# Output products in written order, transposes a token tile later, and a residual added by VectorE

## The chip, the cores and the metric

The kernel runs on one core of a Trainium2 chip. The core has five engines that run their own instruction streams: TensorE (PE in the profile, with PEld for its weight loads), VectorE (DVE), ScalarE (ACT), GpSimd (POOL) and SyncE (SP, which issues most DMAs). They wait for each other by semaphores. The metric is the time of one execution on the device in microseconds (us), a median over several runs. All work is for one sequence of 512 tokens.

## The reference, cut to what matters

An encoder trunk of four layers: gated DeltaNet (GDN), an MLP, gated linear attention (GLA) and a second MLP. After each of them stands a residual sum and a layer normalisation over the 1024 channels.

```python
for i in range(DEPTH):                        # DEPTH = 2
    j = i // N_MIXERS
    if i % N_MIXERS == 0:
        m = _mixer_gdn(x, a_w_in[j], a_conv[j], a_alog[j], a_dt_bias[j], a_norm_g[j], a_w_out[j])
    else:
        m = _mixer_gla(x, b_w_in[j], b_gate_w2[j], b_gate_b[j], b_norm_g[j], b_w_out[j])
    x = _layernorm(DEEPNORM_ALPHA * x + m, ln1_g[i], ln1_b[i])
    x = _layernorm(DEEPNORM_ALPHA * x + _sq_relu_mlp(x, mlp_w1[i], mlp_w2[i]), ln2_g[i], ln2_b[i])
```

Both mixers begin with a product of x with `w_in` (projections), run a recurrence per head in both directions, normalise the head's output, gate it, and end with a product with `w_out` (the output product). The MLP is `relu(x @ w1)**2 @ w2` with 4096 features.

## The kernel before, in words

**Tiles.** The 512 tokens are four token tiles (`NT` = 4) of 128 rows, `xt0` to `xt3`, each 128 x 1024 in fp32. A half tile is 512 of the 1024 columns. Projections want x with channels on the partitions; so each finished token tile is transposed on TensorE: `xpose` (L146) makes two groups (`q` = 0, 1) of four 128x128 transposes, each into one PSUM bank named `tp`; ScalarE copies the bank to `xth` (L149) and VectorE subtracts that copy from the bank into `xtl` (L150). The pair is a high and a low part: an fp32 product is made as three matmuls by `mm3` (L109 high by high, L110 and L111 the cross terms).

**Stages.** In the trace GDN runs from 0 to about 437 us, the first MLP (MLP0) to about 788, GLA to about 1056 and the second MLP (MLP1) to 1401. The transposes at the end of a stage and the first projections of the next are called a seam here. The projections that begin a stage (`proj_halves`) are made in two halves of 256 tokens: all of them for token tiles 0 and 1 first, then for tiles 2 and 3.

**Output product of a mixer.** Most heads' part of the output product is made early and summed with alpha times x into `z` (`out_part`, `out_pieces`; in GLA z lies in the `xt` tiles themselves). The last heads' part is `out_last`: for each token tile and half it opens a bank `ob`, puts z into it with a matmul by the identity (L241, the residual matmul), and adds the products with `w_out`. In GDN these are two heads, 6 and 7, each one `mm3` of 512 columns; in GLA they are two heads of two blocks each, four `mm3`. Head 7 is the last to be ready in GDN: `fo` (L1364, VectorE) is transposed into `otp` (L1368), gated into `p` (L1370), and split in `oh` (L1371, ScalarE) and `ol` (L1372, VectorE). In GLA the last head goes from `o` (L791) by `otp` (L795) to `oth` (L798) and `otl` (L799).

**Layer normalisation.** `layernorm` takes the two half tiles: statistics (L184, L185), the inverse root (L159 to L165, two steps of it on ScalarE), a subtract and multiply for each half (L188), and a multiply and add: on VectorE for the first half (L191), on ScalarE and GpSimd for the second (L193, L194). With `last=True` the second half too is finished on VectorE.

**MLP.** It begins with four features' projections (`specs`, by `proj_halves`), then single ones (`feature`), and has its hidden features in four groups. The last group's product with `w2` is `last`: banks `pl`, eight `mm3` for each half tile, the first four with the high and low parts of one hidden half and the other four with those of the other (`ah`, `al`, made on ScalarE and VectorE at L90 and L91), then the sum into x (L320, VectorE), layernorm, and the transposes for the next stage, into the banks `pj`.

**What sets the order.** A scheduler orders the instructions of each engine by their dependencies and its own estimates, unless a stretch of the program stands under `in_order(engine)`, which chains all instructions of that engine in the order in which they are written. PSUM is divided anew in each stage: GDN has 1 bank `tp`, 2 `ac` and 3 `pj`, GLA 2 `tp`, 2 `ac` and 4 `pj`, the MLPs 2 each of `pj`, `X`, `Y` and `Z`.

Of the kernel before, what the change touches and what calls it, by code (L numbers as in the profile page):

```python
# [8 lines left out]
F32 = mybir.dt.float32  # L9
# [8 lines left out]
P = 128  # L18
# [10 lines left out]
class Ctx:  # L29
# [109 lines left out]
    def xpose(self, t, src, tags=("tp",)):  # L139

        nc = self.nc
        for q in range(2):
            ps = self.bank([P, 4, P], F32, name="tp", tag=tags[(2 * t + q) % len(tags)])
            for i in range(4):
                k = 4 * q + i
                nc.tensor.transpose(ps[:, i, :], src[:, k * P:(k + 1) * P], self.ident)  # L146
            hi = self.xth[:, 4 * q:4 * q + 4, t * P:(t + 1) * P]
            lo = self.xtl[:, 4 * q:4 * q + 4, t * P:(t + 1) * P]
            last = nc.scalar.copy(hi, ps)  # L149
            nc.vector.tensor_tensor(lo, ps, hi.bitcast(F32), ALU.subtract)  # L150
        return last

# [78 lines left out]
    def out_last(self, w, ks, lhs, z, tags, par, homes=None, xtags=("tp",)):  # L231

        nc = self.nc
        homes = iter(homes or [None] * len(ks))
        ws = [[self.wrows(w, k * P, hf * 512, next(homes)) for k in ks[::2]] for hf in range(2)]
        for t in range(NT):
            sl = slice(t * P, (t + 1) * P)
            pss = []
            for hf in range(2):
                ps = self.bank([P, 512], F32, name="ob", tag=tags[(2 * t + hf) % len(tags)])  # L240
                nc.tensor.matmul(ps, self.ident, z[t][hf], start=True, stop=False)  # L241
                for i, k in enumerate(ks):
                    ah, al = lhs(k, sl)
                    wh, wl = ws[hf][i // 2]
                    self.mm3(ps, ah, al, wh[:, i % 2, :], wl[:, i % 2, :], False, i == len(ks) - 1)
                pss.append(ps)
            self.layernorm(pss, self.xh(t), par)
            self.xpose(t, self.xt[t], xtags)


def mlp(c, w1, w2, g, b, out=None, extra=None):
# [13 lines left out]
    with c.banks(pj=2, X=2, Y=2, Z=2), tc.tile_pool(name="mlp", bufs=2) as pool:  # L265
# [133 lines left out]
        def last(gi, h):  # L399

            a = {}
            for i in range(2):
                for j in range(2):
                    a[i, j] = pair(h[j][:, :, HT * i:HT * i + HT], "raw" if i else "ah")
            ws = [c.wrows(w2, (gi * GF + 2 * (i % 4)) * P, i // 4 * 512, pool=ring("w2") if i < 3 else None if i < 6 else ring("raw"))
                  for i in range(8)]
            if out is None:
                c.new_x()
            for t in range(NT):
                sl = slice(t % 2 * P, t % 2 * P + P)  # L410
                for hf in range(2):
                    ps = c.bank([P, 512], F32, name="pl", tag="XYZ"[(2 * t + hf) % 3])
                    for k in range(GF):
                        wh, wl = ws[4 * hf + k // 2]
                        ah, al = a[t // 2, k // HF]
                        c.mm3(ps, ah[:, k % HF, sl], al[:, k % HF, sl], wh[:, k % 2, :], wl[:, k % 2, :], k == 0, k == GF - 1)
                    add(t, hf, ps)
                c.layernorm(c.xh(t), c.xh(t), par, last=out is not None)
                if out is None:
                    c.xpose(t, c.xt[t], ("pj",))  # L420
                else:
                    nc.sync.dma_start(out[t * P:(t + 1) * P, :], c.xt[t])
# [3 lines left out]
        for f, ps in enumerate(c.proj_halves(specs)):  # L426
            act(ps, h[0][:, f, :])
# [80 lines left out]
def gla(c, gc, w_in, gate_w2, w_out, ln_g, ln_b):  # L508
# [5 lines left out]
    with c.banks(ac=2, tp=2, pj=4), tc.tile_pool(name="gla", bufs=2) as pool:  # L514
# [11 lines left out]
        gps, *qk0 = c.proj_halves(specs)  # L526
# [19 lines left out]
        with c.in_order(mybir.EngineType.PE):  # L546
# [18 lines left out]
            for h in range(H):  # L565
                for s in level:
# [12 lines left out]
        c.out_last(w_out, list(range(KT // 2, KT)), lhs, z, ("pj",), par,  # L579
                   [None, (pool, "v", "sr", 2), (pool, "F", "F", 2), (pool, "v", "sr", 2)])  # L580
# [384 lines left out]
def gdn(c, w_in, conv_w, a_log, dt_bias, norm_g, w_out, ln_g, ln_b, x):  # L965
    tc, nc = c.tc, c.nc
    with c.banks(ch=2, pj=3, tp=1, ac=2), tc.tile_pool(name="gdn", bufs=1) as pool:
# [37 lines left out]
        c.out_last(w_out, [6, 7], lhs, z, ("ac", "pj"), par)  # L1005
# [375 lines left out]
def body(tc, nc, a, out):  # L1381
    with contextlib.ExitStack() as es:
# [5 lines left out]
        gdn(c, a["a_w_in"][0], a["a_conv"][0], a["a_alog"][0], a["a_dt_bias"][0], a["a_norm_g"][0],  # L1388
            a["a_w_out"][0], a["ln1_g"][0], a["ln1_b"][0], x)
        with tc.tile_pool(name="gcst", bufs=1) as gp:  # L1390
            gc = []
            mlp(c, a["mlp_w1"][0], a["mlp_w2"][0], a["ln2_g"][0], a["ln2_b"][0],
                extra=lambda tmp: gc.append(GlaConst(c, gp, a["b_gate_b"][0], a["b_norm_g"][0], tmp)))
            gla(c, gc[0], a["b_w_in"][0], a["b_gate_w2"][0], a["b_w_out"][0], a["ln1_g"][1], a["ln1_b"][1])
        mlp(c, a["mlp_w1"][1], a["mlp_w2"][1], a["ln2_g"][1], a["ln2_b"][1], out=out[0])
# [18 lines left out]
```

## Time and profile before

| | |
|---|---|
| median of three runs | 1403.77 us (1403.65 to 1403.82) |
| span of the profiled execution, first to last instruction | 1401.7 us |
| busy TensorE / VectorE / ScalarE / GpSimd in it | 1366.0 / 929.5 / 689.5 / 121.3 us |
| mean granted TensorE clock | 0.998 |
| residual matmuls (L241) | 16 in GDN and 16 in GLA as the trace counts them, two to a half tile |
| transposes of x (L146) | 128 matmuls, 21.0 us shown |

The profiled execution's own time isn't given apart from its span; the median lies 2.1 us over the span, time before the first and behind the last instruction.

How to read the rows. A row of the timeline has the start in us from the span's start, the duration in us, engine, line, operation, output<-inputs, partitions x elements and a count; in brackets stands how long the engine was idle before and what released it. Matmuls are pipelined: each is shown from its start to its modelled end, so successive ones overlap and their distance from start to start is what they cost. A row of the waits has the waiting engine, output and line, what it waited for, us in all, times, and the longest. A row of the windows has the stretch and its length, then the busy time of PE, PEld, DVE, ACT and POOL, each with its count, the granted clock (1.00 is full), the DMA share and GB/s.

### The profile page before, as it was taken

The numbers are of one execution on the slowest core, as the hardware profiler recorded it, in microseconds if no ns is written. First come the engines' busy times: TensorE is split into PE (matmuls) and PEld (weight loads), VectorE is DVE, ScalarE is ACT, GpSimd is POOL, SyncE is SP. The second block draws the span as 40 slices with busy tenths as digits, with TensorE's granted clock in tenths as the row PEclk, the third lists the DMA queues.
The fourth block names the chain that finished last, engine by engine and source line by source line (L and its number), as shares of the span: only waits on it lengthen the run. The fifth ranks groups of instructions, "written<-read, shape, count | busy, mean of one in ns | idle before, by whom it ended". The sixth has DMA issues, their size and how long they took to land.

```text
span 1401.7 us, 20232 instructions
## 1 busy us (share of the span) xinstructions
PE 1366.0 (97%) x7933; PEld 1116.8 (80%) x7933; DVE 929.5 (66%) x1541; ACT 689.5 (49%) x1320; POOL 121.3 (9%) x168
## 2 busy tenths in 40 slices
PE   7999999999999999999999999999999999999997
PEld 6777777777777888888887888888878888888886
DVE  5787787778667365655556577877764655656655
ACT  3776657666633454444543354554433644445430
POOL 5000000000003300100000100000002000001000
PEclk9999999999999999999999999999999999999999
DMA  6212111211133964655431222222217666656121
GB/s 171 76 48 59 46 46 46 61 46 46 47 111 96 291 154 148 144 155 120 105 96 44 85 86 73 61 61 61 89 47 225 178 183 150 165 120 134 48 83 52
DMA packets 153030, 142.23 MB, mean 101 GB/s; under 512 B 8399, under 2 KB 123207, under 8 KB 152935
## 3 DMA queue, kind: packets, MB, share of 16 engines
q1 hardware_dynamic: 144112, 111.49, 26.5%
q0 software_dynamic: 8256, 29.37, 10.8%
q8 instruction: 62, 1.02, 0.3%
q14 instruction: 33, 0.27, 0.1%
q10 hardware_dynamic: 567, 0.08, 0.0%
HBM read 113.66 MB, written 2.10 MB: 83 GB/s over the span
## 4 chain that ended last, share of the span: by engine, by line
PE 59%; issue 23%; DMA 6%; ACT 6%; POOL 3%; DVE 2%; SPq 1%; DVEq 0%; POOLq 0%; ACTq 0%
DMA w2r<-w2r 4%; PE pj L109 3%; PE pj L111 3%; PE pj L110 3%; PE pjv L109 3%; PE pjv L111 3%; PE pjv L110 3%; PE scp L688 2%; DMA w2r<-in_mlp_w 2%; PE op L1345 2%; PE pjq L110 1%; PE pjq L111 1%; PE pjq L109 1%; PE op L776 1%; PE lv L1220 1%
## 5 line engine op out<-in xcount | busy, mean ns | idle before, releaser
L91 DVE TENSOR_TENSOR wl<-wst,wh 128x1024 fp32r<-128x1024 f32 x137 | 168.5, 1230 | 194.0 <-ACT wh L90 193.3
L90 ACT CAST wh<-wst 128x1024 fp32r<-128x1024 f32 x137 | 144.0, 1051 | 282.7 <-PE pj L110 170.2
L109 PE MATMUL pj<-xth,wh 128*128 128x512 f32 (+1 forms) x544 | 202.0, 372 | 1.7 <-ACT h L276 0.9
L111 PE MATMUL pj<-xth,wl 128*128 128x512 f32 (+1 forms) x544 | 201.7, 371 | 0.4 <-DVE wl L91 0.4
L110 PE MATMUL pj<-xtl,wh 128*128 128x512 f32 (+1 forms) x544 | 201.6, 371 | 0.4 <-DVE xtl L150 0.3
L91 DVE TENSOR_TENSOR w2l<-w2r,w2h 128x1024 fp32r<-128x1024 f32 x84 | 102.6, 1221 | 68.3 <-ACT w2h L90 68.3
L109 PEld LDWEIGHTS pj<-xth,wh 128*128 128x128 f32 x544 | 102.2, 188 | 20.4 <-ACT h L276 2.3
L110 PEld LDWEIGHTS pj<-xtl,wh 128*128 128x128 f32 x544 | 102.5, 188 | 18.6 <-DVE xtl L150 0.8
L111 PEld LDWEIGHTS pj<-xth,wl 128*128 128x128 f32 x544 | 102.4, 188 | 18.6 <-DVE wl L91 0.8
L90 ACT CAST w2h<-w2r 128x1024 fp32r<-128x1024 f32 x84 | 88.2, 1050 | 57.2 <-DMA w2r<-in_mlp_w 25.5
L303 POOL DMA_DIRECT2D w2r<-w2r x48 | 41.5, 902 | 398.2 <-DVE w2l L91 230.1
L90 ACT CAST ah<-h 128x1024 fp32r<-128x1024 f32 x40 | 42.1, 1054 | 42.1 <-PE pX L110 16.8
L110 PE MATMUL pX<-w2l,ah 128*128 128x512 f32 x144 | 56.1, 390 | 0.0
L109 PE MATMUL pX<-w2h,ah 128*128 128x512 f32 x144 | 56.1, 390 | 0.0
L111 PE MATMUL pX<-w2h,al 128*128 128x512 f32 x144 | 56.1, 390 | 0.0
L109 PE MATMUL pjv<-wh,xth 128*128 128x512 f32 x128 | 54.9, 429 | 0.0
L91 DVE TENSOR_TENSOR al<-h,ah 128x1024 fp32r<-128x1024 f32 x40 | 48.9, 1222 | 5.3 <-ACT ah L90 3.7
L160 ACT ACTIVATE rsy<-rsv 128x1 f32<-128x1 f32 (+1 forms) x28 | 5.6, 201 | 90.9 <-DVE rsv L159 90.9
L111 PE MATMUL pjv<-wh,xtl 128*128 128x512 f32 x128 | 50.2, 392 | 0.0
L110 PE MATMUL pjv<-wl,xth 128*128 128x512 f32 x128 | 49.9, 390 | 0.0
L1168 POOL TENSOR_TENSOR atl<-on,ath 128x512 f16<-128x512 f32 x16 | 20.9, 1306 | 323.4 <-ACT ath L1167 171.5
L109 PE MATMUL pjk<-xth,wh 128*128 128x512 f32 (+1 forms) x112 | 42.1, 376 | 0.5 <-ACT wh L90 0.5
(439 smaller groups left out, 3443.3 us busy)
## 6 DMA issues: line engine op xcount, KB each, us to landing
wst<-in_mlp_w SPq DMA_DIRECT2D x80, 512.0 KB, 4.0
w2r<-in_mlp_w SPq DMA_DIRECT2D x48, 512.0 KB, 4.3
w2r<-w2r POOLq DMA_DIRECT2D x48, 512.0 KB, 5.6
wst<-in_a_w_in SPq DMA_DIRECT2D x32, 512.0 KB, 4.0
wst<-in_b_w_in SPq DMA_DIRECT2D x32, 256.0 KB, 3.0
wst<-in_a_w_out SPq DMA_DIRECT2D x8, 512.0 KB, 3.8
wst<-in_b_w_in SPq DMA_DIRECT2D x8, 512.0 KB, 3.7
wst<-in_b_w_out SPq DMA_DIRECT2D x8, 512.0 KB, 3.6
```

Source lines behind the costliest of these rows:

```text
L90: nc.scalar.copy(hi, src)
L91: nc.vector.tensor_tensor(lo, src, hi.bitcast(F32), ALU.subtract)
L109: mm(ps, ah, bh, start=start, stop=False, **kw)
L110: mm(ps, ah, bl, start=False, stop=False, **kw)
L111: mm(ps, al, bh, start=False, stop=stop, **kw)
L160: nc.scalar.activation(y, v, AF.Ln)
L303: nc.gpsimd.dma_start(blocks[a + (q,)], blocks[b + (q,)], accum_op=ALU.add)
L688: T.matmul(ps[:, n, :], kh[:, sl], qh[:, sl], start=True, stop=True)
L776: T.matmul(ops, l, r, start=i == 0, stop=i == len(mm) - 1)
L1168: G.tensor_tensor(atl[:, us, :], at, ath[:, us, :], ALU.subtract)
L1220: T.matmul(ps[:, u, :, :], lhs[:, u, :], cols(rhs, u, s, i), start=True, stop=True)
L1345: T.matmul(op[:, n, :], l, r, start=i == 0, stop=i == len(mm) - 1)
```

## The change

1. `out_last` runs under `in_order` for TensorE, in both mixers. A tile's transposes are written `late` tiles later: one tile in GLA, two in GDN. It returns the tiles whose transposes are left (GDN: 2 and 3; GLA: 3). The last tile's layernorm is finished on VectorE.
2. The MLP makes the transposes that are left (`left`) between the projections of its first features, by `between` in `proj_halves`, into the banks `Y` and `Z`: the last tile's before `k` = 0 and 4 of the third feature, an earlier one's before `k` = 4 and 7 of the first, all in the pass over tiles 0 and 1.
3. The MLP's `last` runs under `in_order` for TensorE. In MLP0 the transposes of tile t-1 stand in the middle of tile t's second half; tile 3's stand between the projections of GLA, before `k` = 0 and 4 of `pjk`, and its layernorm is finished on VectorE. MLP1 keeps its stores and has no transposes.
4. In GLA `out_last` is called with `add=True`: no residual matmul, the first product opens the bank, and VectorE adds the bank to z.

The diff, without the signatures that only pass these on:

```diff
-    def proj_halves(self, specs):
+    def proj_halves(self, specs, between=None):
...
+        between = between or {}
...
-            for ps, ((wh, wl), _, _) in zip(out, specs):
+            for i, (ps, ((wh, wl), _, _)) in enumerate(zip(out, specs)):
                 n = wh.shape[-1]
                 for k in range(KT):
+                    if hf == 0 and (i, k) in between:
+                        between[i, k]()
...
+    def xposes(self, t, *tags):
+
+        src = self.xt[t]
+        return [lambda q=q, tag=tag: self.xpose(t, src, (tag,), (q,)) for q, tag in enumerate(tags)]
...
-    def out_last(self, w, ks, lhs, z, tags, par, homes=None, xtags=("tp",)):
+    def out_last(self, w, ks, lhs, z, tags, par, homes=None, xtags=("tp",), add=False, late=1):
...
+        with self.in_order(mybir.EngineType.PE):
+            for t in range(NT):
+                sl = slice(t * P, (t + 1) * P)
+                pss = []
+                for hf in range(2):
+                    ps = self.bank([P, 512], F32, name="ob", tag=tags[(2 * t + hf) % len(tags)])
+                    if not add:
+                        nc.tensor.matmul(ps, self.ident, z[t][hf], start=True, stop=False)
+                    for i, k in enumerate(ks):
+                        ah, al = lhs(k, sl)
+                        wh, wl = ws[hf][i // 2]
+                        self.mm3(ps, ah, al, wh[:, i % 2, :], wl[:, i % 2, :], add and i == 0, i == len(ks) - 1)
+                    if add:
+                        nc.vector.tensor_tensor(z[t][hf], z[t][hf], ps, ALU.add)
+                    pss.append(z[t][hf] if add else ps)
+                self.layernorm(pss, self.xh(t), par, last=t == NT - 1)
+                if t >= late:
+                    self.xpose(t - late, self.xt[t - late], xtags)
+        return [t for t in range(NT - late, NT)]
...
+            with c.in_order(mybir.EngineType.PE):
+                for t in range(NT):
+                    sl = slice(t % 2 * P, t % 2 * P + P)
+                    for hf in range(2):
+                        ps = c.bank([P, 512], F32, name="pl", tag="XYZ"[(2 * t + hf) % 3])
+                        for k in range(GF):
+                            if out is None and t and hf and k == HF:
+                                c.xpose(t - 1, c.xt[t - 1], ("pj",))
...
+                    c.layernorm(c.xh(t), c.xh(t), par, last=out is not None or t == NT - 1)
...
+        between = {}
+        for j, t in enumerate(left):
+            for q, run in enumerate(c.xposes(t, "Y", "Z")):
+                between[(2, 4 * q) if j == len(left) - 1 else (0, 4 + 3 * q)] = run
+        with c.in_order(mybir.EngineType.PE):
+            halves = c.proj_halves(specs, between)
...
-        gps, *qk0 = c.proj_halves(specs)
+        with c.in_order(mybir.EngineType.PE):
+            gps, *qk0 = c.proj_halves(specs, dict(zip(((2, 0), (2, 4)), c.xposes(NT - 1, "tp", "tp"))))
...
+        return c.out_last(w_out, list(range(KT // 2, KT)), lhs, z, ("pj",), par,
+                          [None, (pool, "v", "sr", 2), (pool, "F", "F", 2), (pool, "v", "sr", 2)], add=True)
...
+        return c.out_last(w_out, [6, 7], lhs, z, ("ac", "pj"), par, late=2)
```

In the changed kernel the lines move: L146, L149, L150 become L149, L152, L153; L184 and L188 become L192 and L196; L241 becomes L251; L1364 and L1368 become L1386 and L1390; L791 and L795 become L813 and L817. VectorE's new add is L257.

Where GDN's output product begins, TensorE's instructions stand as follows before (`ob` is a half tile's bank, `z` the residual, `oh3` and `ol_421` head 6, `oh3` with `ol_422` head 7, `otp` the transposes of head 7):

```order
L241 MATMUL ob_5666<-z_5265,ident_70 128x512
...
L111 MATMUL ob_5666<-wh_5656,ol_421 128x512
L241 MATMUL ob_5674<-z_5506,ident_70 128x512
...
L111 MATMUL ob_5674<-wh_5662,ol_421 128x512
L241 MATMUL ob_5717<-z_5265,ident_70 128x512
...
L110 MATMUL ob_5717<-wl_5657,oh3_414 128x512
L1368 MATMUL otp_5631<-ident_70,fo_5629 128x128 x4
L111 MATMUL ob_5717<-wh_5656,ol_421 128x512
L241 MATMUL ob_5725<-z_5506,ident_70 128x512
...
L109 MATMUL ob_5666<-wh_5656,oh3_414 128x512
```

In the changed kernel the same stretch begins so:

```order
L251 MATMUL ob_5666<-z_5265,ident_70 128x512
L109 MATMUL ob_5666<-wh_5656,oh3_414 128x512
L110 MATMUL ob_5666<-wl_5657,oh3_414 128x512
L111 MATMUL ob_5666<-wh_5656,ol_421 128x512
L1390 MATMUL otp_5631<-ident_70,fo_5629 128x128 x4
L109 MATMUL ob_5666<-wh_5656,oh3_414 128x512
L110 MATMUL ob_5666<-wl_5657,oh3_414 128x512
L111 MATMUL ob_5666<-wh_5656,ol_422 128x512
L251 MATMUL ob_5674<-z_5506,ident_70 128x512
```

Four half tiles' residual and head 6 products stood ahead of the first product of head 7; now one half tile's do, and the transposes into `otp` come right behind it.

The transposes of GDN's first token tile (`xt0`, two groups of four) stand like this on TensorE before, inside the products of a later half tile:

```order
L111 MATMUL ob_5776<-wh_5662,ol_422 128x512
L241 MATMUL ob_5819<-z_5265,ident_70 128x512
L146 MATMUL tp_5703<-ident_70,xt0_5650 128x128 x4
L109 MATMUL ob_5819<-wh_5656,oh3_414 128x512
L110 MATMUL ob_5819<-wl_5657,oh3_414 128x512
L111 MATMUL ob_5819<-wh_5656,ol_421 128x512
L109 MATMUL ob_5819<-wh_5656,oh3_414 128x512
L110 MATMUL ob_5819<-wl_5657,oh3_414 128x512
L111 MATMUL ob_5819<-wh_5656,ol_422 128x512
L241 MATMUL ob_5827<-z_5506,ident_70 128x512
L146 MATMUL tp_5710<-ident_70,xt0_5650 128x128 x4
L109 MATMUL ob_5827<-wh_5662,oh3_414 128x512
```

And in the changed kernel, behind tile 2's last product (`ob_5748`):

```order
L111 MATMUL ob_5748<-wh_5662,ol_422 128x512
L149 MATMUL tp_5777<-ident_70,xt0_5650 128x128 x4
L149 MATMUL tp_5784<-ident_70,xt0_5650 128x128 x4
L251 MATMUL ob_5791<-z_5265,ident_70 128x512
L109 MATMUL ob_5791<-wh_5656,oh3_414 128x512
L110 MATMUL ob_5791<-wl_5657,oh3_414 128x512
```

The two groups stood eight instructions apart and now follow each other.

Where GLA's output product begins, TensorE's instructions before (`F` and `v` are the places of other weight halves, `o` the last head's output):

```order
L241 MATMUL ob_10490<-xt0_5650,ident_70 128x512
...
L111 MATMUL ob_10490<-wh_10468,otl_8458 128x512
L241 MATMUL ob_10504<-xt0_5650,ident_70 128x512
...
L111 MATMUL ob_10504<-F_10480,otl_8458 128x512
L795 MATMUL otp_10450<-ident_70,o_10417 128x128
...
L795 MATMUL otp_10457<-ident_70,o_10431 128x128
L241 MATMUL ob_10553<-xt1_5651,ident_70 128x512
L109 MATMUL ob_10490<-v_10474,oth_8457 128x512
```

In the changed kernel:

```order
L109 MATMUL ob_10488<-wh_10466,oth_8441 128x512
...
L111 MATMUL ob_10488<-wh_10466,otl_8442 128x512
L817 MATMUL otp_10448<-ident_70,o_10415 128x128
...
L817 MATMUL otp_10455<-ident_70,o_10429 128x128
L109 MATMUL ob_10488<-v_10472,oth_8441 128x512
```

The residual matmuls are gone, and the second half tile's first six products now stand behind the transposes of `o`.

More of the change, by code (lines that the diff above doesn't have):

```diff
@@ L137, in new_x, with xpose @@
         self.xtl = self.big.tile([P, KT, S], F32R, name="xtl", tag="xtl")
-    def xpose(self, t, src, tags=("tp",)):
+    def xpose(self, t, src, tags=("tp",), qs=(0, 1)):
         nc = self.nc
-        for q in range(2):
+        for q in qs:
             ps = self.bank([P, 4, P], F32, name="tp", tag=tags[(2 * t + q) % len(tags)])
@@ L235, in out_last, with mlp @@
         ws = [[self.wrows(w, k * P, hf * 512, next(homes)) for k in ks[::2]] for hf in range(2)]
[L236 to L251, printed above, removed]
+        with self.in_order(mybir.EngineType.PE):
[17 more added lines that the diff above has]
+        return [t for t in range(NT - late, NT)]
+def mlp(c, w1, w2, g, b, left, out=None, extra=None):
     tc, nc = c.tc, c.nc
@@ L1391, in body @@
             gc = []
[L1392 removed]
+            mlp(c, a["mlp_w1"][0], a["mlp_w2"][0], a["ln2_g"][0], a["ln2_b"][0], left,
                 extra=lambda tmp: gc.append(GlaConst(c, gp, a["b_gate_b"][0], a["b_norm_g"][0], tmp)))
[L1394 to L1395 removed]
+            left = gla(c, gc[0], a["b_w_in"][0], a["b_gate_w2"][0], a["b_w_out"][0], a["ln1_g"][1], a["ln1_b"][1])
+        mlp(c, a["mlp_w1"][1], a["mlp_w2"][1], a["ln2_g"][1], a["ln2_b"][1], left, out=out[0])
 def kernel(**inputs):
```

27 lines of the change are left out of this document (8 added, 19 removed).

## The prediction

> **What bounds the kernel now.** I read the page first (busy shares, the row of the granted clock), then the list of waits on TensorE alone in the three stretches in which a stage ends (417 to 456.6, 737 to 797 and 1020 to 1065 us), then the timeline there.
>
> ```profile
> PE 1366.0 (97%) x7933; PEld 1116.8 (80%) x7933; DVE 929.5 (66%) x1541; ACT 689.5 (49%) x1320; POOL 121.3 (9%) x168
> ...
> PEclk9999999999999999999999999999999999999999
> ```
>
> TensorE is busy 97% of the span at the full clock, so time is won or lost only where it waits, or does work that another engine could do. The waits in the three stretches (us in all, times, longest):
>
> ```profile
> PE tp L146 <- DVE xtl L150: 1.3, 2, 0.7
> PE tp L146 <- DVE rst L164: 1.2, 2, 0.8
> PE pj L109 <- ACT xth L149: 0.7, 1, 0.7
> ...
> PE tp L146 <- POOL xt L194: 2.5, 4, 0.7
> PE pjq L109 <- DVE xt L320: 0.9, 1, 0.9
> ...
> PE tp L146 <- POOL xt L194: 1.8, 4, 0.6
> ...
> PE pj L110 <- DVE xtl L150: 0.3, 1, 0.3
> ```
>
> Such a listed wait is not the whole loss, as the start of the output product of the first MLP shows:
>
> ```profile
> 737.01 0.39 PE L109 MATMUL pl<-w2h,ah 128*128 128x512 f32 x1
> 737.24 0.40 PE L110 MATMUL pl<-w2l,ah 128*128 128x512 f32 x1
> ```
>
> A matmul of 512 columns starts 0.23 us after the one before and is shown 0.39 long, so each listed wait costs 0.16 more. The seams then cost 3.2+5x0.16=4.0 us (GDN to MLP0), 3.4+5x0.16=4.2 (MLP0 to GLA) and 2.1+5x0.16=2.9 (GLA to MLP1). These 11.1 us are all that moving transposes can win.
>
> **The change part by part.** *GDN's output product, now in written order.*
>
> ```profile
> 417.01 1.02 PE L241 MATMUL ob<-z,ident 128*128 128x512 f32 x2
> 418.56 1.02 PE L241 MATMUL ob<-z,ident 128*128 128x512 f32 x2
> ...
> 420.69 0.69 DVE L1364 TENSOR_TENSOR fo<-op,ors 128x512 f32<-128x512 f32 x1
> 421.45 0.64 PE L1368 MATMUL otp<-ident,fo 128*128 128x128 f32 x4
> 422.98 0.62 ACT L1371 CAST oh<-p 128x512 fp32r<-128x512 f32 x1 [4.73 <-DVE p L1370]
> 423.63 0.69 DVE L1372 TENSOR_TENSOR ol<-p,oh 128x512 fp32r<-128x512 f32 x1 [0.69 <-ACT oh L1371]
> 423.66 0.50 PE L109 MATMUL ob<-wh,oh 128*128 128x512 f32 x1
> ```
>
> Until head 7 is ready at 423.66, TensorE now does the residual and head-6 part of four half tiles from 417.01 on, 1.55 us each (417.01 to 418.56). In the new order head 7's transposes stand behind one half tile, and everything behind them waits for them. VectorE's order up to `ol` is unchanged, so `otp` still starts at 421.45 and head 7's product at 423.66. TensorE idles from 418.56 and again behind `otp`, and three half tiles, 3x1.55=4.65 us of work, are left over. The third matmul then also waits for `ol` (to 424.32, against a turn 0.46 behind 423.66). That makes +4.8, with little doubt in it (4.6 to 5.2).
>
> *GDN's transposes.* Removed: the 4.0. Added:
>
> ```profile
> 433.37 0.68 DVE L184 BATCH_NORM_STATS2 bst<-ob 128x6 f32<-128x512 f32 x1
> ...
> 434.82 0.60 PE L146 MATMUL tp<-ident,xt 128*128 128x128 f32 x4
> ...
> 436.03 0.73 DVE L188 SCALAR_TENSOR_TENSOR xt<-ob,bmv,lnp 128x512 f32<-128x512 f32 x1
> 436.69 0.67 DVE L150 TENSOR_TENSOR xtl<-tp,xth 128x512 fp32r<-128x512 f32 x1
> ...
> 437.42 0.66 PE L146 MATMUL tp<-ident,xt 128*128 128x128 f32 x4 [0.61 <-DVE xtl L150]
> ```
>
> This stage has one `tp` bank, so a tile's second four transposes wait until the first four are copied and subtracted. Before, matmuls stood between the two (434.82 to 437.42) and the wait left was 0.7 at most; now, for tile 0, nothing stands there. VectorE decides how long it is: tile 2's statistics and both its L196 stand ahead of that subtraction, 0.68+2x0.73+0.67=2.8 and small steps after tile 2's last matmul, a wait of about 3.1. Tile 1's pair, with one `pj` matmul between and two weight splits in VectorE's way, I put at 2.8. Each can be from 0.7 (as now) to 3.1: 1.4 to 6.2 for both. I take 5.9, near the upper end, because the order sets it and not a chance of timing: net +1.9 (-2.6 to +2.2). Tiles 2 and 3 go between projections that need only tiles 0 and 1: nothing.
>
> *MLP0's first features.* Waits at 457 to 490 us:
>
> ```profile
> PE pj L109 <- ACT h L276: 0.9, 2, 0.6
> PE pj L111 <- DVE wl L91: 0.4, 1, 0.4
> ...
> 483.63 1.05 ACT L90 CAST wh<-wst 128x1024 fp32r<-128x1024 f32 x1 [4.81 <-DMA wst<-in_mlp_w]
> ```
>
> They come from weights that arrive late: 1.3+3x0.16=1.8. TensorE gets there 4.8+1.9=6.7 us later. The loads that crowd these weights start with the last layernorm, which comes later by 4.8+3.1, less two thirds of the removed waits (2.7) and the transposes of two tiles (4x0.44): about 3.4. So the weights gain some 3.3 us on TensorE and most of the wait goes: -1.5 (-1.8 to 0). On SP two more `w2r` loads stand ahead of feature 7's weights; these have the same 3.3 us. In MLP1 the reverse holds, since TensorE comes earlier and the last layernorm does not: +0.5 (0 to 1.8, the same wait).
>
> *MLP0's last product.* Removed: the 4.2, as the transposes now come half a product later; the next stage starts with `gps`, which I leave 0.3 for its first wait. Added: the order no longer hops over late operands.
>
> ```profile
> 740.30 1.22 DVE L91 TENSOR_TENSOR al<-h,ah 128x1024 fp32r<-128x1024 f32 x1 [0.50 <-ACT ah L90]
> ```
>
> The second half's `ah` is there when that row starts, at 740.3, and `al` when it ends, at 741.5. TensorE would want `ah` 12 matmuls behind 737.01, at 739.77, and `al` two or three matmuls behind that: waits of 0.5 and 0.7. Before, other matmuls filled this. Net -4.2+0.3+1.2=-2.7 (-3.6 to -2.5). MLP1 has the same edit without transposes: +1.2 (1.0 to 1.4).
>
> *GLA's output product: the residual on VectorE, and written order.*
>
> ```profile
> 1020.94 1.02 PE L241 MATMUL ob<-xt,ident 128*128 128x512 f32 x2
> ...
> 1024.46 1.67 DVE L791 SCALAR_TENSOR_TENSOR o<-o,rs,sr 128x256 f32<-128x256 f32 x4
> 1025.88 1.07 PE L795 MATMUL otp<-ident,o 128*128 128x128 f32 x8 [0.30 <-DVE o L791]
> 1026.56 1.27 ACT L798 ACTIVATE oth<-otp,gcol 128x512 fp32r<-128x512 f32 x2 [2.93 <-PE otp L795]
> 1027.31 1.40 DVE L799 SCALAR_TENSOR_TENSOR otl<-otp,gcol,oth 128x512 fp32r<-128x512 f32 x2
> ...
> 1038.78 1.02 PE L241 MATMUL ob<-xt,ident 128*128 128x512 f32 x2
> ...
> 1042.42 1.02 PE L241 MATMUL ob<-xt,ident 128*128 128x512 f32 x2
> ...
> 1044.10 0.65 PE L146 MATMUL tp<-ident,xt 128*128 128x128 f32 x4 [0.23 <-POOL xt L194]
> ...
> L320 DVE TENSOR_TENSOR xt<-xt,pl 128x512 f32<-128x512 f32 x16 | 10.9, 684 | 25.5 <-PE pl L111 25.5
> ```
>
> A half tile takes 3.64 us (1038.78 to 1042.42), 12x0.23 of it products: a residual costs 0.86. Two of the eight lie ahead of `otp`, which waits for `o` either way; the other six save 6x0.86=5.2. The second half tile's six early matmuls move behind `otp`: +1.4, with TensorE idle from 1020.94+1.4=1022.3 to 1025.9. Then `oth` (0.6 a half, from 1026.56) and `otl` (to 1028.0) are waited for with nothing beside them: +0.9. The eight adds, 0.68 each, are 5.5 us on VectorE. The transposes' 2.9 goes, but a tile now lasts 24x0.23=5.6, while layernorm takes 5.3 from the tile's last product to the second half's transposes (1038.78 to 1044.10) and has one add, 0.68, more ahead of it: 0.4 short at each of three tiles, and up to 1.2 where VectorE is taken. I take 0.8, in the middle, since VectorE is busy 25 of 35 us there (below): +2.4. Net -5.2+1.4+0.9-2.9+2.4=-3.4 (-5.5 to -1).
>
> *The granted clock.* Stretches of busy time (TensorE first, clock and DMA share last but one):
>
> ```profile
> 436.00:439.41 3.41, 1.96 (x10) 1.04 (x8) 3.41 (x11) 2.24 (x5) 1.19 (x1) 1.00 0.00 0
> 1391.73:1395.14 3.41, 0.81 (x4) 0.35 (x2) 2.45 (x7) 0.41 (x2) 0.00 (x0) 1.00 0.00 0
> 1395.15:1398.56 3.41, 0.00 (x0) 0.00 (x0) 2.47 (x7) 0.00 (x0) 0.00 (x0) 0.50 0.00 0
> 1021.00:1056.00 35.00, 33.46 (x145) 23.89 (x144) 25.47 (x54) 11.49 (x25) 3.79 (x3) 1.00 0.18 48
> ```
>
> After a stretch of 3.41 us with 0.81 us of TensorE work the clock was halved; one with 1.96 kept it. The new idle stretches hold less than 1.96: 418.6 to 423.7 has one `otp` (0.6 of 5.1), 1022.3 to 1025.9 nothing. If the clock is decided by fixed stretches of that length, each idle stretch fills one far enough for a drop in about half of all positions. A drop costs half of the next 3.4 us of work, 1.7; the waits in GDN's transposes may cause more of them (0 to +7 in all). I take one drop of the two, +1.7.
>
> [...]
>
> Sum: 4.8+1.9-1.5+0.5-2.7+1.2-3.4+1.7=+2.5 on a span of 1401.7. The median of the runs is 1403.8, so 2.1 us lie around the span, which stay. Forecast: 1403.8+2.5=1406.3.
>
> **Rivals.** *A, the clock holds.* The idle stretches don't lower the grant: 1406.3-1.7=1404.6. [...] Against it: the end of this trace. *B, faster: head 7's chain sets no wait.* Place: between `op` and `oh` in GDN. If `oh` came by 418.6, where the first half tile's early part ends, instead of 423.6, written order would cost nothing there and the clock would hold: 1406.3-4.8-1.7=1399.8. It decides from about 420.5 on. For it: the chain is 3 us of work spread over 420.3 to 423.6, and an order on TensorE alone can change when VectorE gets its operands. Against it: the rows of this chain all stand ahead of the first changed row on VectorE. *C, VectorE bounds GLA's output.* It is busy 25.5 of 35 us there; with 5.5 more in some 31 us it is full. Then that part wins nothing, and its waits bring one more drop: 1406.3+3.4+1.7=1411.4. For it: the arithmetic. Against it: the adds are spread over four tiles.
>
> **Numbers.** Forecast 0.50 (its own range 1404.6 to 1409.7, none to three drops), A 0.20, B 0.18, C 0.12. About 0.2%, 2.8 us, is what a measurement tells from no change here: slower means above 1406.6, faster below 1401.0. More than half of the forecast's range and all of C lie above: 0.28+0.12=0.40. The rest of the forecast and A are the same: 0.22+0.20=0.42. B is faster: 0.18. The range takes in B's point and leaves out C and what lies beyond B: 1399.5 to 1410.5.
>
> **What would show it.** Right: no residual matmul in GLA; TensorE waiting 2 to 4 us for `fo` and again for `o`; the subtraction ending a wait of 2 to 3 us between GDN's halves; a granted clock under 1.00 behind 421 or behind 1025 us. Wrong: those waits under 1 us, waits of over 1 us at each tile of the MLPs' output products, or a clock of 1.00 all through with the time above 1408.

## The result, and the profile after

The changed kernel takes 1412.2 us (median of 4 runs, 1411.4 to 1412.8) against 1403.7 before: a ratio of 1.0056, 95% interval 1.0044 to 1.0068. It is 8.5 us slower; the forecast was 2.5 slower, and the time lies outside the stated range. The profiled execution has a span of 1410.3 us at a mean clock of 0.992 (before 1401.7 at 0.998).

The page of the changed kernel, busy shares and the row of the clock:

```profile
PE 1364.3 (97%) x7917; PEld 1119.7 (79%) x7917; DVE 934.5 (66%) x1552; ACT 687.4 (49%) x1317; POOL 116.5 (8%) x165
...
PEclk9999999999998999999999999999999999999999
```

TensorE has 16 matmul records less (the residuals of GLA), and the row of the clock has a slice under 9. Its waits at the end of GDN, at MLP0's first features, at the end of MLP0, at GLA's output and at MLP1's first features (the end of MLP1 lists the same two rows as the end of MLP0):

```profile
PE tp L149 <- DVE rst L172: 2.9, 1, 2.9
PE otp L1390 <- DVE fo L1386: 2.7, 1, 2.7
PE ob L109 <- ACT oh L1393: 1.6, 1, 1.6
PE tp L149 <- DVE rst L171: 1.3, 1, 1.3
PE pj L109 <- ACT xth L152: 1.2, 1, 1.2
...
PE pj L111 <- DVE wl L91: 2.1, 1, 2.1
PE pj L110 <- DVE xtl L153: 0.6, 1, 0.6
...
PE pl L111 <- DVE al L91: 0.5, 1, 0.5
PE pl L109 <- ACT ah L90: 0.4, 1, 0.4
...
PE otp L817 <- DVE o L813: 3.4, 1, 3.4
PE tp L149 <- POOL xt L202: 1.5, 3, 0.6
PE ob L109 <- ACT oth L820: 0.3, 1, 0.3
PE tp L149 <- DVE xt L199: 0.2, 1, 0.2
...
PE pj L109 <- ACT h L290: 1.8, 1, 1.8
```

Before, no wait here was over 0.9 us. Now four are over 2: for head 7's `fo`, for the subtraction between the two groups of tile 0's transposes (the list names the small step right behind it, `rst`), for the low part `wl` of weights in MLP0, and for GLA's `o`. The timeline shows the first two of them, and that VectorE's chain to `fo` kept its place (`fo` at 420.69 before):

```profile
418.24 0.40 PE L111 MATMUL ob<-wh,ol 128*128 128x512 f32 x1
421.34 0.66 PE L1390 MATMUL otp<-ident,fo 128*128 128x128 f32 x4 [2.71 <-DVE fo L1386]
423.56 0.79 PE L109 MATMUL ob<-wh,oh 128*128 128x512 f32 x1 [1.56 <-ACT oh L1393]
424.15 0.63 PE L110 MATMUL ob<-wl,oh 128*128 128x512 f32 x1
424.57 0.63 PE L111 MATMUL ob<-wh,ol 128*128 128x512 f32 x1
...
440.54 1.09 PE L149 MATMUL tp<-ident,xt 128*128 128x128 f32 x4 [2.93 <-DVE rst L172]
...
420.59 0.69 DVE L1386 TENSOR_TENSOR fo<-op,ors 128x512 f32<-128x512 f32 x1
...
439.70 0.68 DVE L153 TENSOR_TENSOR xtl<-tp,xth 128x512 fp32r<-128x512 f32 x1
```

The two matmuls behind 423.56 are 0.42 apart, from 424.15 to 424.57, and not 0.23: the clock is halved. It is halved five times ahead of the kernel's end, for 3.41 us each. Each pair of rows is the stretch ahead and the halved one, and the single row at 484.53 is a stretch that no halving follows; TensorE's busy time stands first, the granted clock third from the end:

```profile
419.68:423.09 3.41, 0.66 (x4) 0.42 (x4) 2.21 (x7) 0.20 (x1) 0.00 (x0) 1.00 0.82 228
423.09:426.50 3.41, 2.94 (x6) 1.78 (x6) 1.39 (x2) 0.41 (x1) 0.00 (x0) 0.50 0.22 65
436.74:440.15 3.41, 0.86 (x6) 0.49 (x4) 3.06 (x9) 1.15 (x4) 1.26 (x1) 1.00 0.00 0
440.15:443.56 3.41, 3.02 (x8) 1.93 (x9) 1.90 (x5) 1.31 (x2) 1.26 (x1) 0.50 0.00 0
446.98:450.39 3.41, 0.98 (x6) 0.54 (x4) 3.34 (x10) 1.83 (x4) 0.00 (x0) 1.00 0.49 137
450.39:453.80 3.41, 3.36 (x16) 3.40 (x17) 2.75 (x6) 0.59 (x1) 0.00 (x0) 0.50 0.26 70
484.53:487.94 3.41, 2.04 (x9) 1.70 (x10) 3.41 (x5) 0.20 (x1) 0.20 (x1) 1.00 1.02 217
1030.66:1034.07 3.41, 0.99 (x8) 0.84 (x8) 3.04 (x9) 0.48 (x2) 0.00 (x0) 1.00 0.62 174
1034.07:1037.48 3.41, 3.07 (x8) 2.29 (x8) 1.86 (x4) 0.95 (x2) 0.00 (x0) 0.50 0.43 121
1095.51:1098.92 3.41, 1.60 (x8) 1.02 (x7) 1.88 (x3) 3.35 (x5) 0.00 (x0) 1.00 1.07 252
1098.92:1102.33 3.41, 3.41 (x10) 2.64 (x9) 0.51 (x1) 0.95 (x2) 0.00 (x0) 0.50 1.11 341
```

TensorE works 2.94+3.02+3.36+3.07+3.41=15.8 us in the halved stretches. If that work took half the time at full speed, the halvings cost 7.9 us; matmuls of 512 columns start 0.427 us apart in the halved stretches of this trace and 0.227 elsewhere, and by that they cost 7.4. Both are estimates, and both come to most of the 8.5. They are sums of lost work and leave out what a wait behind a halving takes back. In this trace the halved stretches lie on one raster: 423.09 to 440.15 is 5x3.413, from there to 450.39 3x3.413, to 1034.07 171x3.413, to 1098.92 19x3.413. A stretch with TensorE busy for 1.60 us was followed by a halved one, and one with 2.04 was not.

Where the time went is read from four marks on TensorE: the first matmul of GDN's output product, of MLP0's last product (`pl`), of GLA's output product, of MLP1's last product, and the end of the span. The stretches between them:

| stretch (us) | before | after | difference | of it by halvings, at half their work |
|---|---|---|---|---|
| start to GDN's output | 417.0 | 416.9 | -0.1 | 0 |
| GDN's output to MLP0's last product | 320.0 | 331.2 | +11.2 | 4.7 (three) |
| MLP0's last product to GLA's output | 283.9 | 279.8 | -4.1 | 0 |
| GLA's output to MLP1's last product | 327.6 | 328.0 | +0.4 | 3.2 (two) |
| MLP1's last product to the end | 53.1 | 54.4 | +1.2 | 0 |

By these estimates the change without the halvings is +0.7 to +1.2, close to the +0.8 that the forecast's sum has without its term for the clock.

### The profile page after: what moved, and what is told of

The parts are those of the page before. It is cut to its first block, busy times and chain, and to the rows that moved or that the text cites. A ratio compares the mean times of both kernels' runs of the same rounds, so it can differ in the third digit from the quotient of the medians.

```text
span 1410.3 us, 20196 instructions
## 1 busy us (share of the span) xinstructions
PE 1364.3 (97%) x7917; PEld 1119.7 (79%) x7917; DVE 934.5 (66%) x1552; ACT 687.4 (49%) x1317; POOL 116.5 (8%) x165
```

## The experiments

Two questions: are the halvings really caused by idle TensorE, and what is each part of the change worth? The theory: written order puts whole idle stretches where the scheduler had put other work, and these cost twice, as waits and by the clock behind them. The rivals stand with each run. Times are medians; before, on the chips that ran these, the kernel took 1403.7 to 1404.0.

**Idle stretches filled with work that nobody reads.** `warm` makes n transposes of the identity into a bank of its own.

```diff
+                        if t == 0 and hf == 0 and i == (1 if add else 0):
+                            self.warm(20, "pj" if add else "tp")
...
-                    self.xpose(t - late, self.xt[t - late], xtags)
+                    self.xpose(t - late, self.xt[t - late], xtags, (0,))
+                    if not add:
+                        self.warm(14, "pj")
+                    self.xpose(t - late, self.xt[t - late], xtags, (1,))
```

> The changed kernel with idle TensorE filled by matmuls that nobody reads: 20 transposes of the identity while TensorE waits for fo in GDN and for o in GLA, 14 between the two groups of transposes of GDN's tiles 0 and 1. No wait is shortened. Theory (a stretch of 3.41 us with TensorE busy for less than half of it halves the clock in the next one, at 1.7 us each): four of the five halvings go, 1412.2-4x1.7=1405.4 (1404.5 to 1407.5), and the clock is back at 0.997. Rival (the halved stretches come from the DMA load or another thing and not from idle TensorE): 1412 or more, clock as now.

Measured: 1409.7 us (1408.9 to 1410.8; ratio to before 1.0040, 1.0025 to 1.0055): 2.5 less, where the theory wanted 6.8. None of its runs is as slow as the fastest of the changed kernel, though the intervals of the two ratios overlap, so the trace has to carry the argument. Both halvings at the transposes are gone, GLA's is gone, and MLP1's is gone as well. The one at GDN's front stayed, and a new one came at MLP0's first features:

```profile
420.40:423.81 3.41, 1.45 (x12) 0.97 (x10) 1.93 (x5) 0.52 (x1) 0.00 (x0) 1.00 0.88 258
423.81:427.22 3.41, 3.26 (x6) 1.90 (x7) 1.39 (x2) 0.10 (x1) 0.00 (x0) 0.50 0.09 28
481.84:485.25 3.41, 1.29 (x4) 0.78 (x5) 2.86 (x5) 3.31 (x7) 1.45 (x3) 1.00 1.06 236
485.25:488.66 3.41, 3.41 (x9) 2.65 (x8) 1.95 (x2) 1.67 (x2) 0.00 (x0) 0.50 0.86 264
...
1031.38:1034.79 3.41, 1.91 (x16) 1.44 (x14) 3.25 (x8) 0.69 (x2) 0.00 (x0) 1.00 0.55 151
```

The fill was too small for that position of the raster (1.45 of 3.41). And TensorE came to MLP0's single features 3 us earlier (474.8 instead of 477.8), to operands that did not come earlier, waited for them longer (1.9 and 1.6), and lost the clock there. Where little took the gain back it shows: from GLA's output to MLP1's last product two halvings less made 324.5 us of 328.0, 3.5 against the 3.2 of the estimate, while the wait for `h` there went from 1.8 to 1.0. So useless work on TensorE makes that stretch faster. The rival, with a clock that doesn't depend on idle TensorE, is out: where the fill sufficed the clock held, and in the rows of the changed kernel the stretches ahead of a halving have any DMA share from 0.00 (436.74) to 1.07 (1095.51).

**Written order taken away, one product at a time.** `order=False` leaves the product to the scheduler.

```diff
-        return c.out_last(w_out, [6, 7], lhs, z, ("ac", "pj"), par, late=2)
+        return c.out_last(w_out, [6, 7], lhs, z, ("ac", "pj"), par, late=2, order=False)
```

> The changed kernel, with GDN's output product alone freed from written order (the transposes of tiles 2 and 3 stay in MLP0). Theory: the waits for fo and oh (4.8), most of the waits between the transposes of tiles 0 and 1 (5.9 to about 2) and three halvings (5.1) go: 1412.2-13.8=1398.4, up to 1401 as MLP0's weights are late by more. Rival (head 7's chain moves later too, or the weights take all back): 1408 or more.

Measured: 1403.2 us (1401.2 to 1406.5; ratio 0.9996, 0.9987 to 1.0005): 9.0 less than with the order, where 13.8 were expected. From GDN's output to MLP0's last product it took 323.8 us against 331.2, and before 320.0. What stayed: the transposes still wait for the one bank (2.2 and 0.7), TensorE waits 3.6 us for `wl` in MLP0, and behind each of these places the clock was halved once (mean granted clock 0.72 from 440 to 446 us, 0.84 and 0.88 in the two stretches of 6 us from 476). The profiled execution, at 1405.4 us one of the slower of ten (1401.2 to 1406.5), also lost the clock at 15.8 us and for two stretches in GLA. The mechanism holds; the give-back was undersized.

For GLA's output product the same edit:

```diff
-                          [None, (pool, "v", "sr", 2), (pool, "F", "F", 2), (pool, "v", "sr", 2)], add=True)
+                          [None, (pool, "v", "sr", 2), (pool, "F", "F", 2), (pool, "v", "sr", 2)], add=True, order=False)
```

> The changed kernel, with GLA's output product alone freed from written order, the residual still on VectorE. Theory: the second half tile's matmuls again cover the wait for o (1.4), oth and otl are covered (0.9) and one halving goes (1.7): 1408.2. Rival (VectorE bounds this stretch): within 1 us of 1412.

Measured: 1407.6 us (1407.1 to 1409.5), 4.6 less. GLA's output to MLP1's last product: 322.1 us against 328.0 with the order and 327.6 before. No wait for `o`, `oth` or `otl` is listed, no halving is left in this stretch (the granted clock is 1.00 from 1029 to 1059 us; about 3.2 of the 5.9), and the rival, under 1 us, is out.

For MLP1's last product:

```diff
-            with c.in_order(mybir.EngineType.PE):
+            with c.in_order(mybir.EngineType.PE) if out is None else contextlib.nullcontext():
```

> The changed kernel, with MLP1's last product alone freed from written order. Theory: the waits for ah and al, 1.2 in all, go: 1411.0, and between the first matmul of that product and the end 1.2 us less in the trace. Rival (the end waits for weights either way): no difference there, 1412.2.

Measured: 1410.3 us (1409.7 to 1411.4). From the first matmul of that product to the end the trace has 53.1 us, as before, against 54.4 in every run with the order: the 1.2 us are shown.

**The residual alone.** In written order, and then free:

```diff
-                          [None, (pool, "v", "sr", 2), (pool, "F", "F", 2), (pool, "v", "sr", 2)], add=True)
+                          [None, (pool, "v", "sr", 2), (pool, "F", "F", 2), (pool, "v", "sr", 2)])
```

> The changed kernel, with GLA's residual back on TensorE and written order kept. Theory: eight residuals of 0.86 come back, one of them inside the wait for o, the halving there goes (1.7) and the tiles' transposes wait about 1.7 less: 1412.2+6.0-1.7-1.7=1414.8. Rival (VectorE bounds this stretch, so the adds won nothing): 1412 or less.

Measured: 1415.9 us (1415.2 to 1420.7), 1.1 over the theory; the rival, 1412 or less, is out. GLA's output to MLP1's last product took 329.2 us with one halving, against 328.0 with two: about 2.9 more without the clock. The halving that went is not the one that the theory named: TensorE still waits 2.5 us for `o` and loses the clock at 1037.5, and the one at MLP1's start is gone, where the wait for `h` is 1.0 instead of 1.8.

For the second kernel `order=False` is added to this call.

> The changed kernel, with GLA's output product free from written order and its residual back on TensorE, to price the adds alone. Theory: against 1407.6 with the adds, eight residuals of 0.86 come back, two of them inside the wait for o: +5.2, 1412.8. Rival (VectorE's adds delay each tile's layernorm, so that the transposes' waits eat most of it): +2 or less, under 1409.6.

Measured: 1411.6 us (1409.0 to 1417.1), 4.0 more than free with the adds. Between the two traces 1.2 us of the difference lie between GDN's output and MLP0's last product, where nothing differs: this trace has one more halving there, at 487.2. The stretch itself took 324.7 against 322.1, 2.6 more: between theory and rival. The waits of both, first with the adds, then with the residual matmuls (1018 us to MLP1's first features):

```profile
PE tp L149 <- DVE xt L199: 2.0, 1, 2.0
PE pj L109 <- ACT h L290: 1.5, 1, 1.5
PE tp L149 <- POOL xt L202: 0.5, 2, 0.3
```

```profile
PE pj L109 <- ACT h L290: 0.7, 1, 0.7
PE otp L817 <- DVE o L813: 0.3, 1, 0.3
```

By the forecast's price the eight adds take 5.2 us off TensorE, and 3.0 come back as waits: for a layernorm that is later by the adds, and for `h` at MLP1's start, to which TensorE now comes earlier.

**MLP0's seam alone, and with GLA's.** The first kernel keeps of the change only the written order and the later transposes of MLP0's last product; the second has also the adds and later transposes in GLA, free. GDN's output product is as before in both (`late=0`, free), and MLP1's last product is free. The last lines shown are the first kernel's; the second has `add=True, order=False` there.

```diff
-        return c.out_last(w_out, [6, 7], lhs, z, ("ac", "pj"), par, late=2)
+        return c.out_last(w_out, [6, 7], lhs, z, ("ac", "pj"), par, late=0, order=False)
...
-                          [None, (pool, "v", "sr", 2), (pool, "F", "F", 2), (pool, "v", "sr", 2)], add=True)
+                          [None, (pool, "v", "sr", 2), (pool, "F", "F", 2), (pool, "v", "sr", 2)], late=0, order=False)
```

> Of the change, only the seam from MLP0 to GLA (written order in MLP0's last product, the transposes a tile later, the last ones between GLA's first projections). Theory: 4.1 us less than before: 1399.6. Rival: the late operands of the last product (1.2) and what the seam saved in the changed kernel only thanks to its lateness leave under 1: 1403.

Measured: 1399.7 us (1398.8 to 1401.3; ratio 0.9971, 0.9960 to 0.9982), with 280.0 us from MLP0's last product to GLA's output; every trace with this seam has 279.8 to 280.0.

> Of the change, only the seam from MLP0 to GLA (written order in MLP0's last product, transposes there a tile later) and GLA's sum on VectorE with the transposes a tile later. GDN's output product and transposes as before, GLA's output product free, MLP1's last product free. Theory (the change loses by the waits and halvings of the written order alone): 4.1 us from MLP0's seam and 5.6 from GLA's, as between the traces of before and of the run with GLA free: 1403.7-9.7=1394.0 (1392.5 to 1396). Rival (these gains were there only because TensorE came late from GDN, with more time for loads and splits): 1400 or more.

Measured: 1393.8 us (1393.6 to 1394.5; ratio 0.9928, 0.9915 to 0.9942), with no halving before the end (mean clock 0.998, as before). This beats both kernels, by 9.9 and 18.4 us: the change is worth 10 us where written order doesn't stand against an operand that is late by much. The one place where it is kept, MLP0's last product, waits 0.4 and 0.5 us.

**The wait at MLP0's start.** The idea: in the changed kernel SyncE issues feature 7's weights behind nine `w2r` loads (seven before), at 474.4 us, and they land 14.1 us later, at 488.5. The edit holds SyncE to the order in which the loads are written, six ahead of it and the next two behind.

```diff
-        for f in range(4, GF):
-            feature(0, f, h)
+        with c.in_order(mybir.EngineType.SP):
+            for f in range(4, GF):
+                feature(0, f, h)
...
+            load(0, 1, 0)
```

> The changed kernel, with SyncE held to the written order at the start of each MLP: feature 7's weights are issued behind six w2r loads in all and not behind nine, the next ones in front of the rest. Theory (TensorE's wait for the weights in MLP0 is the queue's order): the wait of 2.1 us there is 0.5 or less, and the time about 2 us less, 1410.2; the same edit may do as much in MLP1 (wait for h, 1.8), down to 1408.5. Rival (the weights wait for a free staging buffer and not behind other loads): the waits stay, 1412.2.

Measured: 1413.0 us (1408.8 to 1418.0), so the time is inconclusive. In the trace, of the fastest of these runs, the wait is gone: MLP0 lists none between 457 and 530 us. Feature 7's weights are issued at 475.9 there, no earlier than before the edit, but land 4.7 us later and not 14.1.

Yet they are not what TensorE waited for in the changed kernel: that wait ended at 485.90, ahead of their landing. It was for `wl` of feature 5, whose weights had landed at 455.6. In the changed kernel VectorE made it only at 484.63, because it stood idle for 8.05 us, until 482.45, for masks (`tmp`) that GpSimd makes for GLA; and GpSimd made these behind the issue of a transfer of its own (`w2r<-w2r`), ahead of which it had waited 2.11 us for another transfer:

```profile
480.86 0.85 POOL L317 DMA_DIRECT2D w2r<-w2r  x1 [2.11 <-DMA w2r<-w2r]
...
482.11 0.31 POOL L498 TENSOR_SCALAR_AFFINE_SELECT tmp<-tmp 128x128 f32<-128x128 f32 x1
...
482.45 0.29 DVE L506 TENSOR_TENSOR mu<-tmp 128x128 uint8<-128x128 f32 x1 [8.05 <-POOL tmp L498]
...
484.63 1.22 DVE L91 TENSOR_TENSOR wl<-wst,wh 128x1024 fp32r<-128x1024 f32 x1
...
485.90 0.50 PE L111 MATMUL pj<-xth,wl 128*128 128x512 f32 x1 [2.05 <-DVE wl L91]
```

Nor is the rival wrong about the issue: in both kernels SyncE issues feature 7's weights 0.03 us after VectorE has read feature 4's out of a staging buffer (474.39 and 475.86). That the order of the loads moves the wait shows against the trace with GLA's output free, where TensorE reaches feature 5 at the same 484.19: `wl` is ready at 487.34 there, with a wait of 2.6, and at 484.26 with the edit. The way from the loads by GpSimd and VectorE is read from the traces; no run takes the masks away. What the edit does to the rest of the kernel isn't settled.

> The fastest kernel so far (1393.8) with the same order on SyncE. Theory: it loses some 1.9 us to late weights at MLP0's start as the kernel before does, and one wait at MLP1's; with both gone 1391.5. Rival: the later w2r loads are late for the first products instead, 1394 or more.

Measured: 1398.8 us (1395.2 to 1402.4), 5.0 more than without the edit. Here TensorE waits 2.2 us for `h` at MLP0's start and 2.8 at MLP1's, and the clock is halved three times (at 481.7, 1055.1 and 1089.3). The rival was right that other loads become late: ScalarE's cast of a `w2r` block, behind which these `h` stand, waits for its load until 475.2 and 1082.9 us, and until 471.5 and 1076.9 without the edit. The order that took the wait at MLP0's start away in the changed kernel (2.1 to none) made it longer here, where TensorE comes earlier (1.2 to 2.2).

> The changed kernel with idle TensorE filled more fully (25 transposes of the identity ahead of head 7's products, 20 ahead of those of GLA's last head and between the groups of tiles 0 and 1) and the same order on SyncE. Theory: no halving is left in GDN, at the start of MLP0 or in GLA, and what the first filled kernel gave back to late weights stays: 1412.2-8.5=1403.7 (1403 to 1406). Rival (late weights do not come from the queue's order): 1408 or more, with TensorE waiting 3 us or more at MLP0's start.

Measured: 1409.4 us (1408.7 to 1411.7), 5.7 more than the theory and in the rival's range, but without the rival's sign, a wait of 3 us or more at MLP0's start (1.5, for `h`). In place the theory holds: at GDN's front, between the transposes, at MLP0's start and in GLA the clock is full (the two rows of GDN's front and GLA's row first), and from GDN's output to MLP0's last product it takes 326.4 us instead of 331.2.

```profile
420.00:423.40 3.40, 3.40 (x25) 2.74 (x24) 3.30 (x8) 1.12 (x2) 0.00 (x0) 1.00 0.21 57
423.40:426.80 3.40, 1.86 (x14) 1.39 (x13) 1.86 (x4) 0.62 (x1) 0.00 (x0) 1.00 0.89 250
...
1029.65:1033.06 3.41, 1.88 (x14) 1.23 (x11) 3.34 (x7) 1.21 (x2) 0.00 (x0) 1.00 0.47 140
...
12.48:15.89 3.41, 1.81 (x15) 1.24 (x12) 3.39 (x6) 3.16 (x6) 0.41 (x2) 1.00 0.55 141
15.89:19.30 3.41, 3.41 (x19) 2.75 (x17) 1.47 (x3) 0.22 (x1) 3.14 (x4) 0.50 0.99 260
```

The rest went elsewhere: MLP1's start lost the clock with a wait of 2.6 for `h` (1.8 before it), and this run lost it once at 15.9 us, ahead of everything that differs, and reached GDN's output 3.0 us later (419.9 against 416.9).

## Why the prediction was wrong, step by step

The four signs that the prediction named for being right all came: no residual in GLA, waits of 2.7 for `fo` and 3.4 for `o`, a subtraction that ends a wait of 2.9 in GDN, and a granted clock under 1.00 behind 421 and 1025 us. So the mechanism of the larger terms was the forecast one. What sank the sum was the size of one term, the clock's; one smaller step was wrong as a mechanism, that of MLP0's first features.

*GDN's front: right.* `otp` at 421.34 and head 7's product at 423.56, against 421.45 and 423.66 forecast. *GDN's transposes: right.* A wait of 2.93+0.16 for tile 0 (3.1 forecast); 1.18 and 1.29 with their 0.16 each for tile 1, 2.8 (2.8 forecast). *MLP0's last product: right in sign, too small,* -4.1 against -2.7: nothing waits at the next stage's start, for which 0.3 was left, and the added waits are 0.4 and 0.5, not 0.5 and 0.7. *MLP1's last product: right,* +1.2. *GLA with MLP1's start: right as a sum.* +0.4 less the 3.2 of two halvings is -2.8, against -3.4+0.5. Its parts were not: MLP1's start waits 1.8 us, the far end of its 0 to 1.8. Two small slips stand in this part of the sum: 24x0.23 is 5.5 and not 5.6, and 3.64-12x0.23 leaves 0.88 for a residual and not 0.86; they move it by some 0.1 us.

*MLP0's first features: wrong in sign,* -1.5 forecast, while the wait grew from 1.8 to 2.1+0.16. The step "the weights gain some 3.3 us on TensorE" failed, because this wait was not for weights on their way: feature 5's had landed 30 us before, and `wl` was late by VectorE's 8.05 us of waiting for GpSimd's masks. The trace before had the same, 8.58 us of it ahead of its 0.4 us wait for `wl`; of its three waits only the 0.6 us for `h` stood directly behind weights that were still landing, those of the row that the prediction shows. Tiles 2 and 3, put at "nothing", cost 0.6+0.16 in a wait for `xtl`. Together GDN's output to MLP0's last product came to +6.5 without its halvings, against 4.8+1.9-1.5=+5.2.

*The granted clock: the step that sank the forecast.* "I take one drop of the two, +1.7" measured five, 7.4 to 7.9 us by the estimates above; the bounds written beside it, 0 to +7, were short too. That is 6 us too little in a forecast that was 6.0 too low. The mechanism was named, and its size came from the wrong bound. The two rows of the trace before, 0.81 of 3.41 (halved) and 1.96 (not), left open what happens between; the forecast used the lower one, and so gave each idle stretch an even chance. In the changed kernel the stretches ahead of a halving held 0.66 to 1.60 us of work, in the last run above one held 1.81, and one with 1.88 kept the clock. An estimate from these rows takes half of the stretch, 1.7 us, as what is needed. Then an idle stretch of 3.4 us or more would cost a halving nearly wherever it lies on the raster: cut by one raster line, its longer part still fills half of one stretch. One of 2.9 us mostly would, and a wait of 1.8 us with others beside it could, as those behind which the halvings at 440.15 and 1098.92 came. By that estimate GDN's front, GLA's wait for `o` and the two waits at the transposes were four halvings to be expected, 6.8 us, and the forecast would have been 1403.8+0.8+6.8=1411.4. Rival A, for which the clock had to hold, fell: none of the stretches ahead of the five halvings was empty, and with 0.66 to 1.60 us of matmuls each was followed by one at a clock of 0.50.

Rival C fell, though its time, 1411.4, is only 0.8 off the measured one; that is luck. Freed from the order, GLA's stretch lost 5.9 us with all eight adds on VectorE, some 3.2 of it by halvings, and the adds only take part of their own gain back. Rival B fell by the rows of head 7's chain, which kept its place.

## What to carry to other kernels

Written order on an engine was worth something here only up to the first operand that came late: behind `fo` and `o` (waits of 2.7 and 3.4 us) everything waited, work that the scheduler had put in between was left over, and the engine's idle time moved into one piece. On TensorE one piece of idle time was dearer here than several small ones: before, with no wait over 0.9 us at these places, the clock stayed at 1.00 there; in the changed kernel five stretches of 3.41 us with 0.66 to 1.60 us of work were each followed by 3.41 us at 0.50. By the estimate above, half of the work in a halved stretch, price such a wait in this kernel at its length and 1.5 to 1.7 us more, or (1.69+3.42)/2=2.6 for two halved stretches in a row (the rows below). And an engine that arrives earlier meets operands that do not (1.9 and 1.6 us of waits at MLP0's start in the first filled kernel): of each gain ahead of a stage's start, ask what the loads, and the engines that split them, will have ready by then. A wait that looks like a late load can be an engine that stands in its own order behind something else, as VectorE did for 8.05 us ahead of feature 5's `wl`.

## What the runs showed of the hardware

No single busy time divides the stretches ahead of a halving from the others in these records, but the range in which both occur is narrow. I laid the raster of each of the thirteen traces (its halved stretches give it) over the trace, from where the clock's records begin (9.3 us before, 10.1 in the changed kernel) to the kernel's end. Of the stretches at full clock, all of some thirty with TensorE busy for under 1.50 us lost the clock in the next one, and none of over 5000 with 1.83 or more did. In the traces of the kernel before and of the changed one, over 800 stretches, the clock was lost behind five, with 0.66 to 1.60 us, and behind none with 1.84 or more. Between 1.50 and 1.83 it went both ways, six of twelve: one with 1.81 lost it (the last pair of rows above), and one with 1.50 kept it, at MLP1's start in the kernel with MLP0's seam alone:

```profile
1087.01:1090.42 3.41, 1.50 (x7) 0.93 (x5) 1.46 (x2) 1.33 (x2) 0.00 (x0) 1.00 1.08 294
1090.42:1093.83 3.41, 3.15 (x14) 2.61 (x15) 1.59 (x2) 2.52 (x5) 0.00 (x0) 1.00 1.09 314
```

What else decides between 1.50 and 1.81 us is open; the shown busy time has modelled ends.

A halved stretch was also followed by another in some traces. At GDN's front this came in four of the traces with written order there, as in the one with GLA's output free, and once in GLA:

```profile
421.86:425.27 3.41, 1.69 (x5) 1.22 (x6) 1.45 (x3) 0.62 (x1) 0.00 (x0) 0.50 0.62 177
425.27:428.69 3.42, 3.42 (x7) 1.95 (x6) 0.80 (x2) 0.00 (x0) 0.00 (x0) 0.50 0.00 0
```

Of 41 halved stretches the five with TensorE busy for 1.57 to 2.54 us were followed by another halved one, and the 36 with 2.94 or more were not. At full clock none with 1.83 or more was, so in these records the two cases differ; the 2.94 of the changed kernel's GDN front is the lowest of the 36. Where the raster lies against the kernel's start differs from trace to trace: counted back by 3.413 us, its first line stands at 2.5 us before and at 3.2 in the changed kernel. The mean clock differs between runs of one kernel too (0.988 to 0.992 in the changed kernel with the loads in order); that the raster's place decides it is an estimate of mine, which no run shows alone.
